# Residual and activation sums by adding transfers on GpSimd's queue, with negated blocks, and a norm into rows of its own

## Chip, cores and metric

The kernel runs on one core of one Trainium2 chip. The metric is the device time of one execution in microseconds (us); less is better. Its engines are TensorE (PE, matrix products; PEld its weight loads), VectorE (DVE), ScalarE (ACT), GpSimd (POOL) and SyncE (SP). Each works through its own instructions in order and waits for the others by semaphores. Transfers (DMA) are issued from the queue of an engine, here nearly all from SP's, and run beside the engines.

## What is computed

One decoder layer on 1024 tokens of width 1024, all in float32. Cut to the part that the change touches:

```python
m = concat([rmsnorm(a, g_attn), rmsnorm(c, g_conv)])
x = x + rmsnorm(m @ w_out, mix_post_norm)
h = rmsnorm(x, ffn_pre_norm)
f = (silu(h @ w_gate) * (h @ w_up)) @ w_down
x = x + rmsnorm(f, ffn_post_norm)
```

Here `a` is the output of an attention with low-rank queries and keys, `c` that of a gated convolution. D_FF is 2816. A last gated embedding is added behind `f`.

## The kernel before

**Precision.** Each float32 matrix is kept as two parts of a reduced type: an upper part (`split`, line 209, a cast on ACT) and the rest (line 210, a subtraction on DVE or POOL). A product is three matmuls: upper with upper, upper with lower, lower with upper. For the output projection these are lines 220 to 222, for the FFN lines 1192, 1194 and 1195.

**FFN products.** The FFN's first two matrix products use a scheme of Strassen's kind. The activations h, transposed, are a 2 x 2 arrangement of blocks of 512 x 512 (128 partitions x 2048 numbers each in memory): B11, B12, B21, B22. The weights of a pair of 128-column tiles form A11 to A22. Seven products per pair and per matrix (gate or up) take the place of eight. `ORDER` is (1, 2, 6, 5, 7, 3, 4), and `RIGHT` names the activation factor of each: product 1 takes B11, 2 B21, 3 B22, 4 T4, 5 T1, 6 T2, 7 T3. The T's are sums of blocks: T3 = B22 - B12, T2 = T3 + B11, T1 = B22 - T2, T4 = B21 - T2. `factor` builds the weight factors, on DVE for the first pair of tiles and on POOL for the others, and splits them. `product` runs 12 matmuls on PE and then gathers the result.

**Rows.** The stage around the change is a loop over t from 0 to 10. `wo_a(t)` finishes the projection of row block t (128 tokens; 24 matmuls), L1071 gathers it, and the square sum (L230 on ACT), the addition of epsilon (L226 on DVE) and the power (L227 on POOL) make the factor of its norm. `wo_x1(t - 1)` multiplies by that factor and the gain (L1077), adds the row block of x that `load_x` had brought (L1079), stores the sum (L1081, tensor x_d) and computes the factor of the second norm. `wo_n(t - 2)` multiplies the same buffer, in place, by that factor and gain (L1086). `h2_turn(t - 3)` transposes the result on PE (L1106, eight per row block; the prediction calls those of row block t "Tt"). For blocks 0 to 3, ACT copies the transposed rows into a buffer (L1108) that goes out to the tensor hr_d (L1116); their B11 and B21 are also split at once. For blocks 4 to 7 the copies (L1110) go into `tr[0]` and `tr[1]`, which are B12 and B22, and B22 is split. At t = 9, B11 and B21 come back from hr_d (L1277, L1278) into the buffers in which the lower parts of T1 and T4 will stand. `raw_load` (L1148) brings the weights, and the first products (1, of the first pair) run once the projection is done.

**Sums.** Behind the loop `t_sum` (L1303) makes the four sums on DVE, each 128 x 2048, and `t_split` splits each, among the weight factors and products that come between.

**What sets the order.** A scheduler with its own model of time puts the instructions of every engine in order; the program's text gives the dependences. Buffers come from two arenas, mem_f (30 units of 128 x 512, raw data) and mem_r (72 units, split data): the free space that has rested longest is given out next, so a load can wait for the last reader of its buffer. Matmul results stand in eight banks.

Of the kernel before, what the change touches and what calls it, by code (L numbers as in the profile page):

```python
# [8 lines left out]
F32 = mybir.dt.float32  # L9
# [126 lines left out]
def hybrid_layer(ctx: ExitStack, tc: tile.TileContext, x, x_t, p_t, cols_in, positions,  # L136
# [69 lines left out]
    def split(h, l, src, gain=None, eng=None):  # L206

        if gain is None:
            act.copy(h, src)  # L209
            (eng or dve).tensor_tensor(l, src, h.bitcast(F32), op=ALU.subtract)  # L210
# [24 lines left out]
    def bank3(ap, k):  # L235
        return ap.rearrange("p (k c) -> p k c", k=k)
# [811 lines left out]

    rows_y, rows_x = {}, {}

    def load_y(t):
        rows_y[t] = mf(2, ML)
        sp.dma_start(rows_y[t].a, y_d[t * P : (t + 1) * P, :])

    def load_x(t):
        rows_x[t] = mf(2, ML)
        sp.dma_start(rows_x[t].a, x[t * P : (t + 1) * P, :])

    def row_norm(t, i):
        r = ss_y[:, 2 * t + i : 2 * t + i + 1]
# [10 lines left out]
        row_norm(t, 0)  # L1073

    def wo_x1(t):
        y, xr = rows_y[t].a, rows_x.pop(t)
        dve.scalar_tensor_tensor(y, y, ss_y[:, 2 * t : 2 * t + 1], g_mix.a, op0=ALU.mult,  # L1077
                                 op1=ALU.mult)
        dve.tensor_tensor(y, y, xr.a, op=ALU.add)  # L1079
        free(xr)  # L1080
        sp.dma_start(x1_d[t * P : (t + 1) * P, :], y)  # L1081
        row_norm(t, 1)

    def wo_n(t):
        y = rows_y[t].a
        dve.scalar_tensor_tensor(y, y, ss_y[:, 2 * t + 1 : 2 * t + 2], g_ffn.a, op0=ALU.mult,  # L1086
                                 op1=ALU.mult)

# [2 lines left out]
    def four(b):  # L1093
        return b.a.rearrange("p (k c) -> p k c", k=4)

    def h2_turn(t):
        src = rows_y.pop(t)
        o = slice(t % 4 * P, (t % 4 + 1) * P)
        first = t < T // 2
        if first:  # L1100
            raw = mf(2, ML)
        for q in range(2):
            ids, b = ps.get()
            for j in range(4):
                k = 4 * q + j
                pe.transpose(b[:, j * P : (j + 1) * P], src.a[:, k * P : (k + 1) * P], ident[:])  # L1106
            if first:
                act.copy(raw.a[:, q * U : (q + 1) * U], b)  # L1108
            else:
                act.copy(four(tr[q])[:, :, o], bank3(b, 4))  # L1110
# [33 lines left out]
    def raw_load(fp, i, where=None):  # L1144

        for m, w in enumerate((w_gate, w_up)):
            raws[fp, m, i] = r = mf(2, where)
            sp.dma_start(r.a, w[2 * fp + i])  # L1148

    def factor(fp, m, p):  # L1150
        eng = pool if fp else dve
        a = raws[fp, m, 0].a
        a11, a12 = a[:, 0:U], a[:, U:]
        if p == 1:
            src = a11
        elif p == 2:
            src = a12
        else:
            b = raws[fp, m, 1].a
            a21, a22 = b[:, 0:U], b[:, U:]  # L1160
            if p == 6:
                eng.tensor_tensor(a21, a21, a22, op=ALU.add)
# [12 lines left out]
        h, l = wp[fp, m, p] = pair(1, RR)
        split(h.a, l.a, src)
        if p == ORDER[-1]:
            free(raws.pop((fp, m, 0)), raws.pop((fp, m, 1)))

# [74 lines left out]
    for t in range(T + 3):  # L1254
        if t < T:
            wo_a(t)
        elif t == T:
            for d in (mTa, wo):
                for h, l in d.values():
                    free(h, l)  # L1260
            for i in head[:2]:
                product(*i)
        elif t == T + 1:
            for i in head[2:]:
                product(*i)
        if 1 <= t <= T:
            wo_x1(t - 1)
        if t < T:
            load_x(t)
        if 2 <= t <= T + 1:  # L1270
            wo_n(t - 2)
        if t == T + 1:
            free(g_mix, g_ffn)
            t2 = mf(4, MG)
            tf["T1"], tf["T4"] = pair(4, BT), pair(4, BT)
            b11, b21 = tf["T1"][1].a.bitcast(F32), tf["T4"][1].a.bitcast(F32)
            sp.dma_start(b11.rearrange("p (k c) -> p k c", k=4), hr_d[:, 0:4, :])  # L1277
            sp.dma_start(b21.rearrange("p (k c) -> p k c", k=4), hr_d[:, 4:8, :])  # L1278
        if t >= 3:
            h2_turn(t - 3)  # L1280
        if t + 2 < T:
            load_y(t + 2)
        if t == T - 1:
            raw_load(0, 1, ML)
        if t == T:
            raw_load(1, 0, ML)
        if t == T // 2:
            for i in head:
                factor(*i)
    b12, b22 = tr[0], tr[1]  # L1290

    def both(f, fp, p):
        for m in range(2):
# [2 lines left out]
    def t_split(n, v):  # L1296
        if n not in tf:
            tf[n] = pair(4, BT)
        h, l = tf[n]
        split(h.a, l.a, v)  # L1300

    def t_sum(o, x, y, op):
        dve.tensor_tensor(o, x, y, op=op)  # L1303
# [314 lines left out]
```

## Time and profile before

| | |
|---|---|
| median of 3 executions | 1226.24 us (1225.47 to 1227.34) |
| the profiled execution | 1227.49 us |
| its span in the profile | 1225.4 us |
| PE busy / DVE busy / POOL busy | 1201.5 / 810.6 / 503.8 us |
| chain that ended last, share of PE | 80% |

The profile comes from one execution. A row of a timeline gives start and duration in microseconds, engine, line, operation, the memory written and read, the size, and in brackets how long the engine stood idle before and which instruction ended that. In the grouped lines the last two entries are the idle time and what ended it. The chain that ended last follows the waits back from the end; a line of the waits view sums what an engine waited for. DMA rows give the median time from issue to landing.

The stage of the loop lies between 436 and 536 us of the span. GpSimd's queue carries no transfer there; all are on SP's queue.

### The profile page before, as it was taken

To read this page: it belongs to the slowest core of one execution; us is meant where nothing else is said; L and a number is where in the kernel's file an instruction comes from. 1 tells how busy PE (TensorE), PEld (TensorE's weight loads), DVE (VectorE), ACT (ScalarE), POOL (GpSimd) and SP (SyncE) were. 2 spreads that over 40 slices of the span, in tenths; PEclk is the share of its full clock that TensorE was granted. 3 is DMA by queue.
4 is the path that set the end of the run, shared out by engine and by line. 5 is a ranking of instruction groups with operands and counts; after the bars stand their busy time and mean duration, and the time that the engine had idled before them with its cause. 6 is when DMAs were issued, how large, how long until landed. Compare 5 with 4: busy or idle time off the path is not lost.

```text
span 1225.4 us, 16706 instructions
## 1 busy us (share of the span) xinstructions
PE 1201.5 (98%) x5918; PEld 1012.2 (83%) x5918; DVE 810.6 (66%) x1173; ACT 587.3 (48%) x1079; POOL 503.8 (41%) x392
## 2 busy tenths in 40 slices
PE   8999999999999999789999999999999999999998
PEld 6998888889999888678788888888888888888886
DVE  6676346478867758785657665565556677758775
ACT  7543333267766736543433333333345546545652
POOL 4433534226554311025888646674634102202321
PEclk8999999999999999889999999999999999999999
DMA  8712553994561667524465445543566576654342
GB/s 267 258 39 104 184 202 133 278 365 90 135 161 44 232 223 252 203 104 143 161 229 197 140 144 190 178 157 118 209 209 200 184 242 230 233 172 164 120 136 79
DMA packets 89821, 217.77 MB, mean 178 GB/s; under 512 B 9030, under 2 KB 18026, under 8 KB 88426
## 3 DMA queue, kind: packets, MB, share of 16 engines
q1 hardware_dynamic: 89392, 216.17, 53.4%
q8 instruction: 46, 0.75, 0.3%
q10 hardware_dynamic: 346, 0.54, 0.2%
q14 instruction: 37, 0.30, 0.1%
HBM read 145.38 MB, written 71.04 MB: 177 GB/s over the span
## 4 chain that ended last, share of the span: by engine, by line
PE 80%; DVE 6%; DMA 5%; issue 3%; ACT 3%; POOL 2%; ACTq 0%; POOLq 0%; DVEq 0%; SPq 0%
PE banks L1192 10%; PE banks L1195 10%; PE banks L1194 10%; PE banks L220 7%; PE banks L222 7%; PE banks L221 7%; PE banks L1391 6%; PE banks L1390 6%; PE banks L1389 6%; PE banks L894 2%; DVE mem_r L210 2%; PE banks L1498 1%; PE banks L1501 1%; PE banks L1500 1%; PE banks L865 1%
## 5 line engine op out<-in xcount | busy, mean ns | idle before, releaser
L210 DVE TENSOR_TENSOR mem_r<-mem_f,mem_r 128x512 fp32r<-128x512 f32 (+1 forms) x404 | 374.4, 958 | 206.4 <-ACT mem_r L209 194.1
L209 ACT CAST mem_r<-mem_f 128x512 fp32r<-128x512 f32 (+2 forms) x407 | 258.4, 666 | 410.6 <-PE banks L1194 128.7
L1192 PE MATMUL banks<-mem_r 128*128 128x512 f32 x616 | 242.0, 393 | 4.5 <-ACT mem_r L209 3.4
L1194 PE MATMUL banks<-mem_r 128*128 128x512 f32 x616 | 241.6, 392 | 0.0
L1195 PE MATMUL banks<-mem_r 128*128 128x512 f32 x616 | 240.8, 392 | 0.1
L220 PE MATMUL banks<-mem_r 128*128 128x512 f32 (+2 forms) x536 | 196.3, 371 | 2.4 <-ACT mem_r L209 1.7
L221 PE MATMUL banks<-mem_r 128*128 128x512 f32 (+2 forms) x536 | 196.4, 368 | 1.3 <-POOL mem_r L210 1.2
L222 PE MATMUL banks<-mem_r 128*128 128x512 f32 (+2 forms) x536 | 196.0, 368 | 0.0
L1192 PEld LDWEIGHTS banks<-mem_r 128*128 128x128 f32 x616 | 116.5, 189 | 30.7 <-ACT mem_r L209 5.0
L1195 PEld LDWEIGHTS banks<-mem_r 128*128 128x128 f32 x616 | 116.7, 189 | 25.7 <-DVE mem_r L210 1.1
L1194 PEld LDWEIGHTS banks<-mem_r 128*128 128x128 f32 x616 | 116.8, 190 | 24.3 <-DVE mem_r L210 0.2
L1391 PE MATMUL banks<-mem_r 128*128 128x512 f32 x308 | 119.8, 389 | 0.0
L1390 PE MATMUL banks<-mem_r 128*128 128x512 f32 x308 | 119.8, 389 | 0.0
L1389 PE MATMUL banks<-mem_r 128*128 128x512 f32 x308 | 119.8, 390 | 0.0
L220 PEld LDWEIGHTS banks<-mem_r 128*128 128x128 f32 x536 | 101.2, 190 | 19.1 <-ACT mem_r L209 2.8
L221 PEld LDWEIGHTS banks<-mem_r 128*128 128x128 f32 x536 | 101.6, 190 | 17.4 <-POOL mem_r L210 1.4
L222 PEld LDWEIGHTS banks<-mem_r 128*128 128x128 f32 x536 | 101.5, 189 | 16.1
L879 POOL TENSOR_TENSOR mem_f<-mem_f,stats 128x640 f32<-128x640 f32 (+5 forms) x64 | 73.4, 1161 | 92.0 <-DVE stats L878 49.4
L227 POOL TENSOR_TENSOR small<-small,mhalf 128x1 f32<-128x1 f32 (+2 forms) x46 | 37.6, 821 | 177.5 <-DVE small L226 177.0
L1210 DVE TENSOR_TENSOR mem_f<-banks,mem_f 128x512 f32<-128x512 f32 x66 | 45.2, 686 | 55.9 <-PE banks L1195 55.8
L210 DVE TENSOR_TENSOR mem_r<-banks,mem_r 128x512 fp32r<-128x512 f32 (+3 forms) x118 | 69.3, 612 | 12.9 <-ACT mem_r L209 12.3
L1390 PEld LDWEIGHTS banks<-mem_r 128*128 128x128 f32 x308 | 57.8, 188 | 12.0
(197 smaller groups left out, 1890.0 us busy)
## 6 DMA issues: line engine op xcount, KB each, us to landing
sc_d<-mem_f SPq DMA_DIRECT2D x77, 256.0 KB, 3.5
mem_f<-sc_d SPq DMA_DIRECT2D x77, 256.0 KB, 3.0
mem_f<-in_w_gate_dram SPq DMA_DIRECT2D x22, 512.0 KB, 5.2
mem_f<-in_w_up_dram SPq DMA_DIRECT2D x22, 512.0 KB, 5.1
mem_f<-in_w_down_dram SPq DMA_DIRECT2D x22, 512.0 KB, 4.5
wc_d<-mem_f SPq DMA_DIRECT2D x22, 512.0 KB, 2.7
mem_f<-wc_d SPq DMA_DIRECT2D x44, 256.0 KB, 3.1
mem_f<-in_w_down_dram SPq DMA_DIRECT2D x33, 256.0 KB, 3.4
```

What stands on the lines that cost most here:

```text
L209: act.copy(h, src)
L210: (eng or dve).tensor_tensor(l, src, h.bitcast(F32), op=ALU.subtract)
L220: pe.matmul(o, wh, vh, start=i == 0, stop=False)
L221: pe.matmul(o, wh, vl, start=False, stop=False)
L222: pe.matmul(o, wl, vh, start=False, stop=i == n - 1)
L879: pool.tensor_tensor(pt.a[:, 0:n], pt.a[:, 0:n], sm.to_broadcast([P, n]), op=ALU.mult)
L1192: pe.matmul(b, wh.a[:, c], th[:, k], start=first and k == 0, stop=False, skip_group_check=True)
L1194: pe.matmul(b, wh.a[:, c], tl[:, k], start=False, stop=False, skip_group_check=True)
L1195: pe.matmul(b, wl.a[:, c], th[:, k], start=False, stop=k == 3, skip_group_check=True)
L1389: pe.matmul(b, ah.a[:, c], bh.a, start=first, stop=False, skip_group_check=True)
L1390: pe.matmul(b, ah.a[:, c], bl.a, start=False, stop=False, skip_group_check=True)
L1391: pe.matmul(b, al.a[:, c], bh.a, start=False, stop=last, skip_group_check=True)
```

## The change

The row of x is no longer loaded and added on DVE. A transfer on GpSimd's queue reads x from the chip's memory and adds it into the row in place. The second norm writes into rows of its own (`rows_n`), and the first buffer is freed behind it. The sums of activation blocks are four adding transfers on the same queue, between buffers on the chip: b11 += b12, b12 += b22, b22 += b11, b21 += b22. An adding transfer only adds, so blocks off the diagonal (B12, B21) are kept as negatives: ACT multiplies by 1 or -1 where it copied. With that, b12 becomes T3, b22 becomes T2, b11 becomes -T1 and b21 becomes -T4. The weight factors of products 4 and 5 are negated as they are split (L1180 on ACT, L1181 on DVE). The buffer `t2` is gone, the row loads of the projection stand elsewhere in the loop, `raw_load` of two weight halves may use fewer units, and the splits stand later in the text.

```diff
@@ rows and norms
-    def load_x(t):
-        rows_x[t] = mf(2, ML)
-        sp.dma_start(rows_x[t].a, x[t * P : (t + 1) * P, :])
...
     def wo_x1(t):
-        y, xr = rows_y[t].a, rows_x.pop(t)
+        y = rows_y[t].a
         dve.scalar_tensor_tensor(y, y, ss_y[:, 2 * t : 2 * t + 1], g_mix.a, op0=ALU.mult,
                                  op1=ALU.mult)
-        dve.tensor_tensor(y, y, xr.a, op=ALU.add)
-        free(xr)
+        pool.dma_start(y, x[t * P : (t + 1) * P, :], accum_op=ALU.add)
         sp.dma_start(x1_d[t * P : (t + 1) * P, :], y)
         row_norm(t, 1)
 
+    rows_n = {}
+
     def wo_n(t):
-        y = rows_y[t].a
-        dve.scalar_tensor_tensor(y, y, ss_y[:, 2 * t + 1 : 2 * t + 2], g_ffn.a, op0=ALU.mult,
-                                 op1=ALU.mult)
+        y = rows_y.pop(t)
+        rows_n[t] = mf(2, ML)
+        dve.scalar_tensor_tensor(rows_n[t].a, y.a, ss_y[:, 2 * t + 1 : 2 * t + 2], g_ffn.a,
+                                 op0=ALU.mult, op1=ALU.mult)
+        free(y)
@@ h2_turn
-        src = rows_y.pop(t)
+        src = rows_n.pop(t)
...
+            f = -1.0 if q == first else 1.0
             if first:
-                act.copy(raw.a[:, q * U : (q + 1) * U], b)
+                act.mul(raw.a[:, q * U : (q + 1) * U], b, f)
             else:
-                act.copy(four(tr[q])[:, :, o], bank3(b, 4))
+                act.mul(four(tr[q])[:, :, o], bank3(b, 4), f)
@@ factor
-        split(h.a, l.a, src)
+        if p in (4, 5):
+
+            act.mul(h.a, src, -1.0)
+            dve.scalar_tensor_tensor(l.a, src, -1.0, h.a.bitcast(F32), op0=ALU.mult,
+                                     op1=ALU.subtract)
+        else:
+            split(h.a, l.a, src)
@@ the loop over t
-        if t + 2 < T:
-            load_y(t + 2)
+        if 1 <= t < T - 1:
+            load_y(t + 1)
         if t == T - 1:
-            raw_load(0, 1, ML)
+            raw_load(0, 1, ((0, 18),))
         if t == T:
-            raw_load(1, 0, ML)
+            raw_load(1, 0, ((0, 18),))
@@ the sums
-    t_sum(b12.a, b22.a, b12.a, ALU.subtract)
+
+    for o, v in ((b11, b12), (b12, b22), (b22, b11), (b21, b22)):
+        pool.dma_start(o, v, accum_op=ALU.add)
     both(factor, 1, 1)
     both(product, 1, 1)
-    t_sum(t2.a, b12.a, b11, ALU.add)
-    t_split("T3", b12.a)
-    free(b12)
-    raw_load(2, 0)
     both(factor, 1, 2)
     both(product, 1, 2)
-    t_split("T2", t2.a)
-    both(factor, 0, 6)
-    t_sum(b22.a, b22.a, t2.a, ALU.subtract)
+    raw_load(2, 0)
+    t_split("T3", b12)
     both(factor, 2, 1)
     both(product, 2, 1)
-    t_split("T1", b22.a)
-    free(b22)
     both(factor, 2, 2)
     both(product, 2, 2)
+    t_split("T2", b22)
+    both(factor, 0, 6)
+    t_split("T1", b11)
     both(factor, 0, 5)
-    t_sum(t2.a, b21, t2.a, ALU.subtract)
     factor(0, 0, 7)
-    t_split("T4", t2.a)
-    free(t2)
+    t_split("T4", b21)
+    free(*tr.values())
```

Three places show the order in which instructions now stand. First DVE around the norm of row block 6 and the second multiplication of row block 7. Before, with L1077 and L1079 of block 7 and L1086 of block 6; L1162, L1163 and L1171 are sums of up weights for product 6 of the first pair:

```order
L1077 SCALAR_TENSOR_TENSOR mem_f<-mem_f,small 128x1024
L210 TENSOR_TENSOR mem_r<-banks,mem_r 128x4x128
L1210 TENSOR_TENSOR mem_f<-banks,mem_f 128x512
L1079 TENSOR_TENSOR mem_f<-mem_f 128x1024
L1210 TENSOR_TENSOR mem_f<-banks,mem_f 128x512
L1214 TENSOR_TENSOR mem_f<-mem_f 128x512
L1086 SCALAR_TENSOR_TENSOR mem_f<-mem_f,small 128x1024
L226 TENSOR_SCALAR small<-small 128x1
L1162 TENSOR_TENSOR mem_f<-mem_f 128x512
L1163 TENSOR_TENSOR mem_f<-mem_f 128x512
L1171 TENSOR_TENSOR mem_f<-mem_f 128x512
L210 TENSOR_TENSOR mem_r<-mem_f,mem_r 128x512 x2
```

The same place on DVE now. L1164, L1165 and L1173 are the same sums for the gate weights, which now come second, L226 belongs to block 7's first norm or block 6's second, L1074 is block 7's multiplication, L1085 the norm of block 6:

```order
L226 TENSOR_SCALAR small<-small 128x1
L1164 TENSOR_TENSOR mem_f<-mem_f 128x512
L226 TENSOR_SCALAR small<-small 128x1
L1074 SCALAR_TENSOR_TENSOR mem_f<-mem_f,small 128x1024
L1165 TENSOR_TENSOR mem_f<-mem_f 128x512
L1085 SCALAR_TENSOR_TENSOR mem_f<-mem_f,small 128x1024
L1173 TENSOR_TENSOR mem_f<-mem_f 128x512
L1218 TENSOR_TENSOR mem_f<-banks,mem_f 128x512
```

The second set of weight sums stood behind block 6's norm and block 7's multiplication. Its first row now stands ahead of both, so it must have its weights before the two rows go on.

Second, SP's queue at the same place. Here L1077 stores a row of the residual sum (row block 5 first), L1118 stores block 3 to hr_d, L1150 behind it loads the gate weights that the L1164 above reads, into the buffer that the hr_d stores read, and L1284 and L1285 bring hr_d back:

```order
L1077 DMA x_d<-mem_f 128x1024
L1118 DMA hr_d<-mem_f 1024x1x128
L1150 DMA mem_f<-in_w_gate_dram 128x1024
L1284 DMA mem_r<-hr_d 128x2048
L1285 DMA mem_r<-hr_d 128x2048
L1077 DMA x_d<-mem_f 128x1024
L1150 DMA mem_f<-in_w_up_dram 128x1024
L1150 DMA mem_f<-in_w_gate_dram 128x1024
L1077 DMA x_d<-mem_f 128x1024
```

Before, this load of gate weights stood ahead of the hr_d stores of blocks 2 and 3 (L1116), in a buffer that no such store reads:

```order
L1081 DMA x_d<-mem_f 128x1024
L1148 DMA mem_f<-in_w_gate_dram 128x1024
L1116 DMA hr_d<-mem_f 1024x1x128
L1081 DMA x_d<-mem_f 128x1024
L1055 DMA mem_f<-y_d 128x1024
L1116 DMA hr_d<-mem_f 1024x1x128
L1059 DMA mem_f<-in_x_dram 128x1024
L1277 DMA mem_r<-hr_d 128x2048
```

Third, the sums. POOL's queue from the last rows of x on, where L1076 is the adding transfer of a row and the four L1311 are the sums that make -T1, T3, T2 and -T4; behind them stands the first of the sums of the down weights:

```order
L1076 DMA mem_f<-in_x_dram 128x1024
L227 TENSOR_TENSOR small<-small,mhalf 128x1 x3
L1076 DMA mem_f<-in_x_dram 128x1024
L227 TENSOR_TENSOR small<-small,mhalf 128x1
L1311 DMA mem_r<-mem_f 128x2048
L1311 DMA mem_f<-mem_f 128x2048
L1311 DMA mem_f<-mem_r 128x2048
L1311 DMA mem_r<-mem_f 128x2048
L1248 TENSOR_TENSOR mem_f<-mem_f 128x512
```

And DVE where the lower parts of the sums are made; the rows of 128x2048 are those of T3, T1 (in place) and T2:

```order
L1222 TENSOR_TENSOR mem_f<-mem_f 128x512
L210 TENSOR_TENSOR mem_r<-mem_f,mem_r 128x2048
L210 TENSOR_TENSOR mem_r<-mem_f,mem_r 128x512
L210 TENSOR_TENSOR mem_r<-mem_r 128x2048
L210 TENSOR_TENSOR mem_r<-mem_f,mem_r 128x512
L210 TENSOR_TENSOR mem_r<-mem_f,mem_r 128x2048
```

The four sums have moved from DVE to POOL's queue, one behind the other, and T1's lower part stands ahead of T2's, where T2's came first.

More of the change, by code (lines that the diff above doesn't have):

```diff
@@ L1047, in hybrid_layer @@
     brow(ffn_pre_norm, D, g_ffn)
-    rows_y, rows_x = {}, {}
+    rows_y = {}
     def load_y(t):
@@ L1267, in hybrid_layer @@
             wo_x1(t - 1)
-        if t < T:
-            load_x(t)
+        if t == T:
+            free(g_mix)
         if 2 <= t <= T + 1:
@@ L1272, in hybrid_layer @@
         if t == T + 1:
-            free(g_mix, g_ffn)
-            t2 = mf(4, MG)
+            free(g_ffn)
             tf["T1"], tf["T4"] = pair(4, BT), pair(4, BT)
@@ L1289, in hybrid_layer @@
                 factor(*i)
-    b12, b22 = tr[0], tr[1]
+    b12, b22 = tr[0].a, tr[1].a
     def both(f, fp, p):
@@ L1300, in t_split @@
         split(h.a, l.a, v)
-    def t_sum(o, x, y, op):
-        dve.tensor_tensor(o, x, y, op=op)
-    t_sum(b12.a, b22.a, b12.a, ALU.subtract)
+    for o, v in ((b11, b12), (b12, b22), (b22, b11), (b21, b22)):
+        pool.dma_start(o, v, accum_op=ALU.add)
     both(factor, 1, 1)
     both(product, 1, 1)
-    t_sum(t2.a, b12.a, b11, ALU.add)
-    t_split("T3", b12.a)
-    free(b12)
-    raw_load(2, 0)
     both(factor, 1, 2)
     both(product, 1, 2)
-    t_split("T2", t2.a)
-    both(factor, 0, 6)
-    t_sum(b22.a, b22.a, t2.a, ALU.subtract)
+    raw_load(2, 0)
+    t_split("T3", b12)
     both(factor, 2, 1)
     both(product, 2, 1)
-    t_split("T1", b22.a)
-    free(b22)
     both(factor, 2, 2)
     both(product, 2, 2)
+    t_split("T2", b22)
+    both(factor, 0, 6)
+    t_split("T1", b11)
     both(factor, 0, 5)
-    t_sum(t2.a, b21, t2.a, ALU.subtract)
     factor(0, 0, 7)
-    t_split("T4", t2.a)
-    free(t2)
+    t_split("T4", b21)
+    free(*tr.values())
     facc = []
```

## Prediction

> **What bounds the kernel now.** The page's busy times come first.
>
> ```profile
> PE 1201.5 (98%) x5918; PEld 1012.2 (83%) x5918; DVE 810.6 (66%) x1173; ACT 587.3 (48%) x1079; POOL 503.8 (41%) x392
> ```
>
> TensorE (PE) is busy for 1201.5 of 1225.4 us, so taking work off VectorE (DVE) pays only where PE waits or runs slowly. The windows view shows where: start and end, length, busy time and count of PE, weight loads, DVE, ACT and POOL, then granted clock, DMA share and GB/s.
>
> ```profile
> 486.00:496.00 10.00, 10.00 (x48) 8.28 (x48) 8.99 (x12) 7.01 (x13) 1.27 (x3) 1.00 0.60 176
> 496.00:506.00 10.00, 2.66 (x13) 2.07 (x12) 5.47 (x9) 1.99 (x4) 0.87 (x1) 0.72 1.01 385
> 506.00:516.00 10.00, 9.66 (x40) 7.70 (x39) 8.20 (x10) 6.30 (x12) 0.06 (x1) 0.76 0.44 163
> 516.00:526.00 10.00, 6.88 (x29) 5.07 (x28) 10.00 (x10) 6.61 (x7) 0.00 (x0) 0.92 0.17 53
> 526.00:536.00 10.00, 10.00 (x35) 7.98 (x34) 8.77 (x7) 5.31 (x7) 0.00 (x0) 0.74 0.07 28
> 536.00:546.00 10.00, 10.00 (x46) 8.29 (x45) 7.75 (x8) 4.93 (x9) 3.38 (x3) 1.00 0.48 157
> ```
>
> Until 496 and after 536 PE is full at clock 1.00. Between them it loses time twice, and runs at 0.72 to 0.92 in and after each gap. PE's timeline has both (start, duration, what it waited for):
>
> ```profile
> 494.65 0.39 PE L1195 MATMUL banks<-mem_r 128*128 128x512 f32 x1
> ...
> 497.37 0.39 PE L1195 MATMUL banks<-mem_r 128*128 128x512 f32 x1
> 505.09 1.94 PE L1106 MATMUL banks<-ident,mem_f 128*128 128x128 f32 x8 [7.34 <-issue]
> 507.37 0.79 PE L1192 MATMUL banks<-mem_r 128*128 128x512 f32 x1 [0.34 <-ACT mem_r L209]
> 507.96 0.63 PE L1194 MATMUL banks<-mem_r 128*128 128x512 f32 x1
> ...
> 511.78 1.03 PE L1106 MATMUL banks<-ident,mem_f 128*128 128x128 f32 x8
> 512.57 0.48 PE L1192 MATMUL banks<-mem_r 128*128 128x512 f32 x1
> ...
> 525.31 0.79 PE L1192 MATMUL banks<-mem_r 128*128 128x512 f32 x1 [3.09 <-ACT mem_r L209]
> 525.90 0.63 PE L1194 MATMUL banks<-mem_r 128*128 128x512 f32 x1
> 526.33 0.63 PE L1195 MATMUL banks<-mem_r 128*128 128x512 f32 x1
> ...
> 536.14 0.39 PE L1192 MATMUL banks<-mem_r 128*128 128x512 f32 x1
> ```
>
> At full clock matmuls start 0.227 apart (12 from 494.65 to 497.37); behind the gaps 0.43 apart (525.90 to 526.33), for 8 matmuls after the first and 13 after the second. The first gap ends with the transposes of row block 6 (T6, 505.09), those of block 7 (T7) follow at 511.78; the second is a late weight cast. Together that is about 16 us: 7.3 + 0.3 + 3.1 waited, 21 x 0.2 = 4.2 for slow matmuls, 1.94 - 0.79 = 1.1 for slow transposes. Product 6, the first reader of T2, begins at about 536.1. All later matmuls are the same work, so **the sum compares the moment when product 6 can run**.
>
> Why T6 is late stands on DVE's timeline:
>
> ```profile
> 478.01 1.28 DVE L1077 SCALAR_TENSOR_TENSOR mem_f<-mem_f,small 128x1024 f32<-128x1024 f32 x1 [0.66 <-POOL small L227]
> 494.31 1.28 DVE L1077 SCALAR_TENSOR_TENSOR mem_f<-mem_f,small 128x1024 f32<-128x1024 f32 x1 [0.67 <-POOL small L227]
> 496.71 1.22 DVE L1079 TENSOR_TENSOR mem_f<-mem_f 128x1024 f32<-128x1024 f32 x1
> 503.71 1.28 DVE L1086 SCALAR_TENSOR_TENSOR mem_f<-mem_f,small 128x1024 f32<-128x1024 f32 x1 [4.39 <-DMA x_d<-mem_f]
> 504.97 0.68 DVE L1162 TENSOR_TENSOR mem_f<-mem_f 128x512 f32<-128x512 f32 x1
> 508.56 1.28 DVE L1086 SCALAR_TENSOR_TENSOR mem_f<-mem_f,small 128x1024 f32<-128x1024 f32 x1
> 513.86 2.29 DVE L1303 TENSOR_TENSOR mem_f<-mem_f 128x2048 f32<-128x2048 f32 x1 [0.77 <-ACT mem_f L1110]
> ```
>
> Block 6's norm (L1086, in place) waited 4.39 us for the store of the row that it overwrites. Block 7's, queued behind, came at 508.56. The four activation sums are L1303, the first at 513.86.
>
> **The change part by part.** Durations of this stage come from the grouped lines (busy, mean ns), landings from the DMA issues of 430 to 540 (count, KB, median us), where three rows are of the whole span: wc_d, sc_d and wo_d.
>
> ```profile
> L1079 DVE TENSOR_TENSOR mem_f<-mem_f 128x1024 f32<-128x1024 f32 x8 | 9.7, 1218 | 0.0
> L230 ACT ACTIVATE mem_r<-mem_f 128x1024 fp32r<-128x1024 f32 x16 | 17.0, 1063 | 25.4 <-DVE mem_f L1071 20.7 <-DVE mem_f L1079 4.7
> L230 ACT ACTIVATION_READ_ACCUMULATOR mem_r<-mem_f 128x1 f32 x16 | 3.0, 187 | 0.0
> L210 DVE TENSOR_TENSOR mem_r<-mem_f,mem_r 128x2048 fp32r<-128x2048 f32 x4 | 9.1, 2285 | 1.6 <-ACT mem_r L209 1.6
> L209 ACT CAST mem_r<-mem_f 128x2048 fp32r<-128x2048 f32 x4 | 7.6, 1910 | 1.9 <-DVE mem_f L1303 1.9
> mem_f<-in_x_dram SPq DMA_DIRECT2D x7, 512.0 KB, 4.1
> hr_d<-mem_f SPq DMA_DIRECT2D x4, 512.0 KB, 6.4
> mem_f<-in_w_gate_dram SPq DMA_DIRECT2D x3, 512.0 KB, 5.3
> mem_f<-in_w_up_dram SPq DMA_DIRECT2D x4, 512.0 KB, 8.0
> wc_d<-mem_f SPq DMA_DIRECT2D x22, 512.0 KB, 2.7
> sc_d<-mem_f SPq DMA_DIRECT2D x77, 256.0 KB, 3.5
> mem_r<-wo_d SPq DMA_DIRECT2D x4, 1024.0 KB, 12.7
> ```
>
> *Removed.* Eight L1079 (9.7 us) and four L1303 (2.29 each, 9.2 us) leave DVE, eight x loads leave SP's queue, and the norm no longer waits for the row's store. None of the 18.9 us is PE's: it counts only through T6, T7 and T2.
>
> *Negatives.* ACT's copies become multiplications by -1 of the same size, and in the weight splits of products 4 and 5 a subtract becomes a scalar-tensor-tensor. Like forms show no price: L1077 with a scalar and a gain, 1.28, against L1079's 1.22. I take nothing, 0.06 each at most.
>
> *The adding transfers are not in the trace of before.* The x add (512 KB, name its landing A) reads x and the row and writes the row. From below it costs what a load of this size does, 4.1, or 2.7 on a quiet queue (wc_d); a gain over that is excluded, as it moves no less. From above stands the slowest group of this size in the stage, w_up's 8.0, and more if transfers collide. I take half as much again as the quiet copy for the second read, 4.1, times 4.1/2.7 for this stage's traffic: 6.2; **A = 6.5** with the issue. An activation sum (1 MB in SBUF, landing S) has below it 4.1 (2.7 and another 512 KB at 1.4), above it wo_d's 12.7. With the second read, another 2.8, S = 6.9, and **S = 7.1** with the issue: nearer the low end, because the DMA share there is 0.17 and 0.07, not 1.01.
>
> The Trainium skill, "Collectives: The Full Stack", section "The bandwidth ceiling: the fold count and why AG ≠ RS ≠ AR", says that an adding transfer reads two sources through one ring and halves the rate (62.28 against 32.35 GB/s). By that ratio, as an estimate, S would be 4.1 x 1.93 = 7.9 and the sum 2.4 us more. No run here shows it.
>
> *Rows.* Row 5's L1077 stood at 478.01; without the adds ahead of it its successor comes 0.9 earlier, 477.1. It ends at 478.4, its add lands at 484.9, and SP, in order, issues the row's store and then the hr_d store of block 3 at 485.4. A weight load (gate, half 1) has that store's buffer: 485.4 + 6.4 = 491.8, + 5.3 = 497.1. On DVE its first sum (L1164, 0.68 as L1162) stands ahead of the rstd of block 6 and of row 7's L1074: that starts at 497.9, where before it was at 494.31. Behind it L1165 and block 6's norm: 497.9 + 1.28 + 0.68 + 1.28 = 501.1 for T6, **4.0 earlier** than 505.09. Row 7's add is issued at 499.2; in the stretch with DMA share 1.01 I give it 7.0, landed 506.2. Square 1.06 + 0.19, rstd 0.8 (GpSimd's half is the wait of 0.67 ahead of 494.31) and norm 1.28 make 509.5: T7 starts **2.3 earlier**. PE, however, has run dry before T7 (T6 until 503.0, then the 12 matmuls that took 507.37 to 511.78 before, 4.4, until 507.5), so its eight transposes cost 1.9, like T6's, not 0.8: end 511.4 against 512.57, 1.2 earlier.
>
> *Sums.* Each needs the one before it, so all four stand in a chain on GpSimd's queue. Block 7's copies on ACT release the first at 511.1. They land at 518.2, 525.3, 532.4 and 539.5. T2 is the third. DVE takes the lower part of T1 first, in place in the buffer that the third sum reads, then a weight piece, then T2's: 532.4 + 2.2 + 0.6 + 2.2 = 537.4. Before, T2 was an L1303 at 516.67 and a split behind it. GpSimd (0.00 busy from 516 to 536) is blocked meanwhile and loses nothing. ACT's casts of T1 and T3 wait for sums 1 and 2 with weight casts behind them, done by 520.8 and 527.9, where PE wants them at 522.7 and 530.7.
>
> *Sum.* After T7, 94 matmuls at 0.227 take 21.3, with 1.6 for slow ones: PE is at product 6 at 534.3, does two matmuls on T2's upper part and stands until 537.4. As a start of product 6 that is 536.9, **0.8 behind** 536.1. The wait, 2.6, is like the one of 3.09 after which 13 matmuls took 0.2 too much each, so I add the same **2.6**. The second gap of before (late weights) goes, since those loads start behind T5 to T7. In all +3.4: 1227.49 becomes 1230.9 for a profiled execution; these are 1.25 above the median, so 1226.24 + 3.4 = **1229.6**.
>
> **The rivals.**
>
> *Cheap adds.* With A = S = 4.1 row 5's add lands at 482.5, the weights at 494.7, L1074 of row 7 starts at 495.5, T6 at 498.7 and T7 at 505.0; the sums give T2 at 505.6 + 12.3 + 5 = 522.9, before PE needs it at 505.9 + 22.3 = 528.2. That is 8 before 536.1: **1218**. For it: the queue is nearly empty after 516. Against: a second read must be paid somewhere.
>
> *Dear adds (slower).* T2 comes at three times S behind T7, and S beyond about 6.2 goes to the end threefold. S = 9.5 gives 3.4 + 7.2, **1237**; S = 12.7, 3.4 + 16.8, **1246**. For it: wo_d's row. Against: that row's traffic came out of HBM beside others.
>
> *GpSimd's issue is held up by DVE.* GpSimd and DVE already stand in each other's way where both read SBUF:
>
> ```profile
> 542.46 1.80 POOL L1240 TENSOR_TENSOR mem_f<-mem_f 128x512 f32<-128x512 f32 x1 [36.41 <-DVE mem_r L210]
> 544.35 1.29 POOL L1241 TENSOR_TENSOR mem_f<-mem_f 128x512 f32<-128x512 f32 x1
> ```
>
> ```profile
> 544.43 1.76 DVE L210 TENSOR_TENSOR mem_r<-mem_f,mem_r 128x512 fp32r<-128x512 f32 x1
> ```
>
> DVE's L210, a size that took 0.68 in L1162, took 1.76 until GpSimd's L1241 was done, and L1240 took 1.80 against 1.29. If an issue waits for the running DVE operation, at most 2.29, then at DVE's load of 8 to 10 tenths about 1 each, three ahead of T2: 3.4 + 3, **1233**. The Trainium skill, "SBUF — State Buffer", section "SBUF: two separate sides", has that rule: GpSimd's writing of descriptors stands still while DVE holds the shared port. No row here shows it for a DMA.
>
> *An even trade.* With S at 6.2 or less, and A as forecast, T2 is in time (511.1 + 18.6 + 5 = 534.7) and product 6 runs at 534.3, 1.8 before 536.1: **1224.4**, within the 0.2%.
>
> **How the numbers follow.** The forecast with its neighbours (A 6 to 7.5, S 6.6 to 8.5) has 0.34, even trade 0.14, cheap 0.24, dear 0.20, held up 0.08. The range goes from the cheap adds, 1217, to the dear ones' end, 1246. A measurement of this kernel tells 0.2%, 2.45 us, from no change: faster is below 1223.8, slower above 1228.7. Faster gets cheap, 0.05 of even trade and 0.01 of the forecast: 0.30. Same gets the rest of even trade, 0.09, 0.10 of the forecast and 0.01 of held up: 0.20. Slower gets dear, 0.23 of the forecast and 0.07 of held up: 0.50.
>
> **What would show it.** T6 and T7 at 501 and 509, an x add of 6.5 and a sum of 7.1 in the DMA issues, and a wait of PE at 534.7 for L210 of T2. If sums land in under 5, no PE wait stands there; if DVE holds issues up, the gap between two sums is longer than their landings. The forecast is wrong above all if S is: 1 us of it is 3 us of the end.

## The result and the profile after

The changed kernel takes 1238.81 us in the median of 5 runs (1237.57 to 1241.15) beside 1226.24 (1225.47 to 1227.48) before: ratio 1.0103, 95% interval 1.0089 to 1.0118. It is **12.6 us slower**; the forecast was 3.4, in a range to 1246. The profiled execution took 1238.81, its span is 1237.0.

The busy times of the page after, to be read against those of before:

```profile
PE 1202.1 (97%) x5918; PEld 1012.2 (82%) x5918; DVE 795.2 (64%) x1161; ACT 587.6 (48%) x1079; POOL 516.6 (42%) x404
```

DVE lost 15.4 us of work, TensorE has the same amount, and the span grew by 11.6: what was freed was not what the end waited for. The windows view (columns as before) shows where:

```profile
466.00:476.00 10.00, 8.44 (x45) 6.67 (x44) 5.08 (x8) 2.30 (x4) 1.99 (x3) 1.00 1.02 269
476.00:486.00 10.00, 8.91 (x42) 6.87 (x41) 6.31 (x9) 6.31 (x13) 2.87 (x4) 1.00 0.94 283
486.00:496.00 10.00, 6.14 (x24) 4.61 (x23) 7.67 (x12) 6.40 (x13) 2.83 (x4) 0.80 0.97 240
506.00:516.00 10.00, 2.62 (x16) 2.06 (x14) 4.46 (x8) 3.10 (x7) 1.06 (x2) 0.83 0.95 306
536.00:546.00 10.00, 7.66 (x32) 5.56 (x30) 6.94 (x5) 5.56 (x8) 0.86 (x1) 1.00 0.78 157
```

Before, PE was full until 496. Now it waits from 466 on. The DMA engines are busy for 1.02, 0.94, 0.97 and 0.95 of the stretches at 466, 476, 486 and 506 (0.96, 0.91, 0.60 and 0.44 before), and DVE, which was at 8.2 to 9.0 of 10 there, is at 4.5 to 7.7: it waits too. PE's timeline around the transposes of blocks 6 and 7 and at product 6:

```profile
507.59 1.03 PE L1106 MATMUL banks<-ident,mem_f 128*128 128x128 f32 x8
517.04 0.80 PE L1200 MATMUL banks<-mem_r 128*128 128x512 f32 x1 [8.42 <-ACT mem_r L209]
517.64 0.63 PE L1202 MATMUL banks<-mem_r 128*128 128x512 f32 x1
518.07 1.91 PE L1106 MATMUL banks<-ident,mem_f 128*128 128x128 f32 x8
...
543.84 0.51 PE L1200 MATMUL banks<-mem_r 128*128 128x512 f32 x1 [1.18 <-ACT mem_r L209]
544.84 0.49 PE L1200 MATMUL banks<-mem_r 128*128 128x512 f32 x1 [0.49 <-ACT mem_r L209]
547.10 0.80 PE L1202 MATMUL banks<-mem_r 128*128 128x512 f32 x1 [1.77 <-DVE mem_r L210]
```

T6 is at 507.59 (forecast 501.1) and T7 at 518.07 (forecast 509.5). Product 6 would have begun at 546.65, had its first two matmuls not gone ahead (547.10 less two of 0.227): 10.5 behind the 536.1 of before, where the forecast had 0.8. Of the 11.6 by which the span grew, about 1 more is slow matmuls behind that last wait. What product 6 waited for stands on ACT, the cast of T2, and on DVE, where T1's lower part goes ahead of T2's:

```profile
541.88 1.91 ACT L209 CAST mem_r<-mem_f 128x2048 fp32r<-128x2048 f32 x1 [4.24 <-DMA mem_f<-mem_r]
```

```profile
541.95 2.29 DVE L210 TENSOR_TENSOR mem_r<-mem_r 128x2048 fp32r<-128x2048 f32 x1 [2.42 <-DMA mem_f<-mem_r]
```

The landings of the DMA issues, in the stretch 430 to 560, with the two queues above them (packets, MB, share of 16 engines):

```profile
q1 hardware_dynamic: 8955, 18.69, 41.8%
q0 software_dynamic: 1728, 8.39, 34.7%
...
mem_f<-in_x_dram POOLq DMA_DIRECT2D x8, 512.0 KB, 6.1
...
mem_r<-hr_d SPq DMA_DIRECT2D x2, 1024.0 KB, 8.9
mem_r<-mem_f POOLq DMA_DIRECT2D x2, 1024.0 KB, 6.9
```

Both estimates of a landing were near: 6.1 in the median for an x add (6.5 with its issue), 6.9 for a sum (7.1). The median hides what decides: the single rows. GpSimd's timeline shows when each transfer was issued,

```profile
460.49 0.89 POOL L1076 DMA_DIRECT2D mem_f<-in_x_dram  x1 [1.88 <-DVE mem_f L1074]
466.66 0.88 POOL L1076 DMA_DIRECT2D mem_f<-in_x_dram  x1 [1.86 <-DVE mem_f L1074]
...
505.97 0.88 POOL L1076 DMA_DIRECT2D mem_f<-in_x_dram  x1 [0.15 <-issue]
...
520.05 0.89 POOL L1311 DMA_DIRECT2D mem_r<-mem_f  x1 [3.70 <-ACT mem_f L1112]
527.61 0.86 POOL L1311 DMA_DIRECT2D mem_f<-mem_f  x1 [6.67 <-DMA mem_r<-mem_f]
534.90 0.86 POOL L1311 DMA_DIRECT2D mem_f<-mem_r  x1 [6.43 <-DMA mem_f<-mem_f]
542.14 0.86 POOL L1311 DMA_DIRECT2D mem_r<-mem_f  x1 [6.38 <-DMA mem_f<-mem_r]
```

and ACT's the square sums (L230) and copies that waited for landings:

```profile
470.32 1.06 ACT L230 ACTIVATE mem_r<-mem_f 128x1024 fp32r<-128x1024 f32 x1 [4.39 <-DMA mem_f<-in_x_dram]
...
476.29 0.60 ACT L1110 ACTIVATE mem_f<-banks 128x512 f32<-128x512 f32 x1 [2.19 <-DMA hr_d<-mem_f]
...
478.21 1.09 ACT L230 ACTIVATE mem_r<-mem_f 128x1024 fp32r<-128x1024 f32 x1
...
514.36 1.06 ACT L230 ACTIVATE mem_r<-mem_f 128x1024 fp32r<-128x1024 f32 x1 [4.80 <-DMA mem_f<-in_x_dram]
...
516.36 2.19 ACT L209 CAST mem_r<-mem_f 128x512 fp32r<-128x512 f32 x4
```

Row 2's add, issued at 460.49, landed at 470.2: 9.7 us. SP, in order, stored that row and only then sent block 0's rows out:

```profile
470.25 0.32 SPq L1077 DMA_DIRECT2D x_d<-mem_f  x1
470.62 0.58 SPq L1118 DMA_DIRECT2D hr_d<-mem_f  x1
...
473.19 0.32 SPq L1077 DMA_DIRECT2D x_d<-mem_f  x1
```

Block 1's copy on ACT (476.29) waited for that hr_d store, because all four blocks go out through one buffer, and the square sum of row 3, landed by 473.2, stood behind the copy until 478.21. Row 7's add took from 505.97 to 514.36, 8.4, among the reloads of hr_d; four weight casts (516.36) stand behind its square sum on ACT, and these are PE's 8.42 us. In both of these adds the first part was standing still. From 460.6 to 464.3 and from 506.2 to 510.0, behind the two issues, the DMA view shows no packet of GpSimd's queue, q0, but SP's queue at work:

```profile
q1 hardware_dynamic: 211, 0.80, 77.9%
```

```profile
q1 hardware_dynamic: 258, 1.26, 93.2%
```

The adds of rows 4 to 6, which landed 5.4 to 5.8 after their issue, moved their first packets about 1.6 after it; those of rows 2 and 7 about 4.1 after it.

DVE's timeline shows where the multiplications (L1074) of rows 5 and 7 stood, and the wait of L1164 for the gate weights ahead of row 7:

```profile
482.81 1.29 DVE L1074 SCALAR_TENSOR_TENSOR mem_f<-mem_f,small 128x1024 f32<-128x1024 f32 x1 [0.66 <-POOL small L227]
...
503.47 0.69 DVE L1164 TENSOR_TENSOR mem_f<-mem_f 128x512 f32<-128x512 f32 x1 [4.13 <-DMA mem_f<-in_w_gate_dram]
...
504.14 1.28 DVE L1074 SCALAR_TENSOR_TENSOR mem_f<-mem_f,small 128x1024 f32<-128x1024 f32 x1
```

### The profile page after: what moved, and what is told of

Read it like the earlier page. It is cut to its first block, busy times and chain, and to the rows that moved or that the text cites. A ratio compares the mean times of both kernels' runs of the same rounds, so it can differ in the third digit from the quotient of the medians.

```text
span 1237.0 us, 16728 instructions
## 1 busy us (share of the span) xinstructions
PE 1202.1 (97%) x5918; PEld 1012.2 (82%) x5918; DVE 795.2 (64%) x1161; ACT 587.6 (48%) x1079; POOL 516.6 (42%) x404
## 3 DMA queue, kind: packets, MB, share of 16 engines
q0 software_dynamic: 1728, 8.39, 3.6%
## 4 chain that ended last, share of the span: by engine, by line
PE 77%; DMA 9%; issue 5%; DVE 4%; ACT 3%; POOL 2%; SPq 0%; POOLq 0%; DVEq 0%; ACTq 0%
PE banks L1203 10%; PE banks L1200 10%; PE banks L1202 10%; PE banks L220 6%; PE banks L221 6%; PE banks L222 6%; PE banks L1391 6%; PE banks L1390 6%; PE banks L1392 6%; PE banks L894 2%; DMA hr_d<-mem_f 1%; PE banks L1502 1%; ACT mem_r L209 1%; PE banks L1501 1%; PE banks L1499 1%
## 5 line engine op out<-in xcount | busy, mean ns | idle before, releaser
L210 DVE TENSOR_TENSOR mem_r<-mem_f,mem_r 128x512 fp32r<-128x512 f32 (+1 forms) x358 | 327.9, 949 | 173.7 <-ACT mem_r L209 163.2
L209 ACT CAST mem_r<-mem_f 128x512 fp32r<-128x512 f32 (+1 forms) x361 | 227.8, 665 | 347.1 <-PE banks L1202 82.2
L1200 PEld LDWEIGHTS banks<-mem_r 128*128 128x128 f32 x616 | 117.1, 190 | 40.1 <-ACT mem_r L209 15.6
L1202 PEld LDWEIGHTS banks<-mem_r 128*128 128x128 f32 x616 | 117.3, 190 | 26.8 <-DVE mem_r L210 2.3
L1203 PEld LDWEIGHTS banks<-mem_r 128*128 128x128 f32 x616 | 116.8, 190 | 24.4 <-DVE mem_r L210 0.3
L220 PEld LDWEIGHTS banks<-mem_r 128*128 128x128 f32 x536 | 100.8, 189 | 22.9 <-ACT mem_r L209 3.2
L221 PEld LDWEIGHTS banks<-mem_r 128*128 128x128 f32 x536 | 101.3, 189 | 17.1 <-POOL mem_r L210 1.3
L222 PEld LDWEIGHTS banks<-mem_r 128*128 128x128 f32 x536 | 101.1, 189 | 16.2
L210 DVE TENSOR_TENSOR mem_r<-banks,mem_r 128x512 fp32r<-128x512 f32 (+3 forms) x118 | 69.5, 613 | 17.2 <-ACT mem_r L209 16.6
L1181 DVE SCALAR_TENSOR_TENSOR mem_r<-mem_f,mem_r 128x512 fp32r<-128x512 f32 x44 | 43.1, 987 | 43.4 <-ACT mem_r L1180 43.4
```

The costliest lines, as they stand in the source:

```text
L220: pe.matmul(o, wh, vh, start=i == 0, stop=False)
L221: pe.matmul(o, wh, vl, start=False, stop=False)
L222: pe.matmul(o, wl, vh, start=False, stop=i == n - 1)
L1200: pe.matmul(b, wh.a[:, c], th[:, k], start=first and k == 0, stop=False, skip_group_check=True)
L1202: pe.matmul(b, wh.a[:, c], tl[:, k], start=False, stop=False, skip_group_check=True)
L1203: pe.matmul(b, wl.a[:, c], th[:, k], start=False, stop=k == 3, skip_group_check=True)
```

## The experiments

Each edit is to the changed kernel where nothing else is said, and each ratio is to the kernel before on the same chip. Lines of the kernels differ by a few.

**e1: x on DVE, sums as transfers.**

```diff
-        pool.dma_start(y, x[t * P : (t + 1) * P, :], accum_op=ALU.add)
+        xr = rows_x.pop(t)
+        dve.tensor_tensor(y, y, xr.a, op=ALU.add)
+        free(xr)
...
+        if t < T:
+            load_x(t)
```

> The changed kernel, but the row of x is loaded on SP's queue and added on DVE as before; the four sums stay adding transfers. Theory A (the loss of 12.6 us is made by the rows: each x add lands late, the residual's store waits for it on SP's queue, and the hr_d stores, the weight loads and ACT's copies stand behind): the transposes of block 7 come back from 518 to 510 or earlier and the time to 1226-1231. Theory B (the chain of four sums at 7.3 us makes the loss): little changes, 1235-1239. Either way PE waits about 2 to 4 us for T2 if the transposes come early.

1228.37 us, ratio 1.0030 (1.0017 to 1.0043). T7 came at 505.8. PE then waited for T2:

```profile
534.04 1.22 PE L1206 MATMUL banks<-mem_r 128*128 128x512 f32 x2 [4.31 <-ACT mem_r L209]
537.30 0.79 PE L1208 MATMUL banks<-mem_r 128*128 128x512 f32 x1 [2.04 <-DVE mem_r L210]
```

**e2: sums on DVE, x as transfers.**

```diff
-    for o, v in ((b11, b12), (b12, b22), (b22, b11), (b21, b22)):
-        pool.dma_start(o, v, accum_op=ALU.add)
+    t_sum(b12, b12, b22)
+    t2 = mf(4)
...
+    t_sum(t2.a, b12, b11)
...
+    t_sum(b22, t2.a, b22, ALU.subtract)
...
+    t_sum(t2.a, b21, t2.a)
```

> The changed kernel, but the four sums are DVE operations again, with one buffer more, placed as before; the x adds stay transfers. Theory A: T6 and T7 stay at 507 and 518 and the time stays at 1233-1238, 1 to 5 us better than the changed kernel. Theory B: 1224-1228.

1234.82 us, ratio 1.0080 (1.0059 to 1.0102), T7 at 517.4: almost where it is with the sums as transfers, as theory A had it. The time is 0.0023 under the changed kernel's, with overlapping intervals.

**e3: both on DVE** (the edits of e1 and e2).

> The changed kernel with both additions on DVE again, so that only the norm into rows of its own, the negatives and the moved loads are left. If the two kinds of adding transfer are all of the loss, 1218-1227, under before by up to what the norm's wait of 4.39 us held back. If the moved loads and the one buffer for all hr_d stores are part of it without any adding transfer, over 1228.

1222.04 us, ratio 0.9977 (0.9966 to 0.9988), T7 at 505.8. So the norm into rows of its own, the negatives and the moved loads together gain about 2.8 us; the x adds cost 0.0103 of the time from there (e2), the sums 0.0053 (e1), both together 0.0126. T7 stands in the same place in e1 and e3, and in e2 and the changed kernel: the x adds make T7 late, the sums act only behind it.

**e4: plain copies.**

```diff
-        pool.dma_start(y, x[t * P : (t + 1) * P, :], accum_op=ALU.add)
+        pool.dma_start(y, x[t * P : (t + 1) * P, :])
...
-        pool.dma_start(o, v, accum_op=ALU.add)
+        pool.dma_start(o, v)
```

> The changed kernel with each of the twelve adding transfers turned into a plain copy of the same size on the same queue, so the additions of x and of the activation sums are left out. If the second read makes the adding transfers slow, a 1 MB copy lands in 4 to 5 us instead of 6.9 and the x rows in 4 instead of 6.1, and the time falls to 1220-1229. If GpSimd's queue and its issue are slow in themselves, copies land as late as adds and the time stays above 1235.

1225.32 us, ratio 1.0005 (0.9993 to 1.0016), T7 at 510.6. The DMA rows of e4, 430 to 560:

```profile
q0 software_dynamic: 1728, 8.39, 19.2%
...
mem_f<-in_x_dram POOLq DMA_DIRECT2D x8, 512.0 KB, 5.2
...
mem_r<-mem_f POOLq DMA_DIRECT2D x2, 1024.0 KB, 4.8
```

Both kinds of addition are left out here. Queue, bytes and the order on every engine are the same. It is adding that costs: the same 8.39 MB take 34.7% of the engines as adds and 19.2% as copies, 1.81 times as much. By row, the copies of x landed in 3.9 to 7.2, the adds in 5.4 to 9.7.

**e5: four buffers for hr_d.**

```diff
-            raw = mf(2, ML)
+            raw = tr[t // 2].a[:, t % 2 * 2 * U : (t % 2 * 2 + 2) * U]
```

> The changed kernel with one edit: the transposed rows of blocks 0 to 3, which all went out to hr_d through one buffer, get four buffers of their own (the space where blocks 4 to 7 are written later). Theory A1 (each of ACT's copies waits for the hr_d store of the block before, and the square sums of the next rows stand behind it on ACT, so the rows come every 7.65 us and not every 6.2; the gate weights then wait for the same buffer): ACT's 6.3 us of waits for hr_d and DVE's 4.1 for the weights go, block 6's norm (505.9) comes 5 to 8 earlier, and the time falls by 5 to 9 us to 1229-1234 beside 1226. Theory A2 (the landing of the x adds alone paces the rows): under 2 us of change.

1242.57 us, ratio 1.0133 (1.0106 to 1.0159), T7 at 519.7: no faster than the changed kernel (the intervals overlap), against A1. ACT's waits for hr_d went in blocks 0 to 3 (one of 4.8 came up at block 4, which is written into the same space), and PE stays full until 476, but with more transfers at once each lands later. Windows view and DMA rows of e5:

```profile
466.00:476.00 10.00, 10.00 (x49) 8.34 (x49) 7.65 (x11) 6.74 (x15) 2.64 (x5) 1.00 1.03 276
```

```profile
mem_f<-in_x_dram POOLq DMA_DIRECT2D x8, 512.0 KB, 7.0
...
hr_d<-mem_f SPq DMA_DIRECT2D x4, 512.0 KB, 8.2
```

The x adds take 7.0 instead of 6.1, the hr_d stores 8.2 instead of 6.1, and the rows are no earlier in the end.

**e6: the residual's store on ACT's queue.**

```diff
-        sp.dma_start(x1_d[t * P : (t + 1) * P, :], y)
         row_norm(t, 1)
+        act.dma_start(x1_d[t * P : (t + 1) * P, :], y)
```

> The changed kernel with the residual's store issued from ACT's queue behind the square sum that waits for the same add, so that SP's queue is not held up by an x add. If the hold-up of SP (the first hr_d store stood 4.7 us behind it) is the cost: 4 to 6 us off, 1232-1235. If the one buffer's turn (hr_d store 6.1 and two copies 1.5) sets the pace of 7.65 by itself: under 3 us off.

1237.18 us, ratio 1.0083 (1.0060 to 1.0107), T7 at 515.4: 0.0020 or 2.5 us under the changed kernel, with overlapping intervals, as the second theory had it; but e5 speaks against that theory's reason, since four buffers gave nothing back. The x adds landed in 7.4.

**e7: e5 and e6 together.**

> Both edits, four hr_d buffers and the residual's store on ACT's queue, with all twelve adds still transfers. If buffer and queue order are all that the x adds cost, T6 and T7 come as I forecast (501 and 509.5) or earlier and what is left is the wait for T2: 1226-1231. If the adds' landings are left as a cost, 1231-1236.

1242.31 us, ratio 1.0132 (1.0108 to 1.0155), T7 at 520.2. A miss of both theories: neither buffers nor the queue's order give the time back.

**e8: e3 with four hr_d buffers.**

> Both additions on DVE (as in e3), norm in rows of its own, negatives, and four hr_d buffers. If the single buffer costs nothing without the adds, the time of e3 (0.2% under before); if it holds rows up there too, 2 to 5 us less, 1217-1221 beside 1226.

1220.48 us, ratio 0.9951 (0.9932 to 0.9970), T7 at 504.8. Where no adding transfer is in the rows, the same edit as in e5 does no harm: about 3 us under e3, with intervals that just meet. **This version beats both kernels.**

**e9: without the residual's stores.**

```diff
-        sp.dma_start(x1_d[t * P : (t + 1) * P, :], y)
         row_norm(t, 1)
...
-        sp.dma_start(j.a, x1_d[t * P : (t + 1) * P, :])
+        sp.dma_start(j.a, x[t * P : (t + 1) * P, :])
```

> The changed kernel without the eight stores of the residual rows (the end of the kernel reads x in their place, so that the second residual lacks the first one): all twelve adds stay. New theory, after e5: the DMA engines themselves are full between 456 and 506 (shares of 0.82 to 1.02), and an adding transfer takes 1.8 times a copy's share of them, so taking away any 4 MB of other transfers gives the loss back, whichever queue or buffer they use. Then x adds land in 5 or less (6.1 now), PE's waits of 1.2 to 2.1 ahead of the row blocks' matmuls go, and the time falls by 5 to 10 us, ratio 1.002 to 1.006. If the adds' own latency paces the rows, or the buffers do, it stays over 1.008.

1231.25 us, ratio 1.0041 (1.0026 to 1.0056), T7 at 510.7: 0.0062 or 7.6 us come back, as expected, but not through the landings: the median is 6.4, and the adds of rows 3, 4, 5 and 7 landed in 9.1, 8.0, 7.4 and 9.2, each later than in the changed kernel (6.5, 5.8, 5.4 and 8.4). Row 2's add is followed by row 4's 13.9 us later (459.39 and 473.29 on GpSimd) instead of 16.0, and row 7's is issued at 497.71, not 505.97. The edit takes away two things at once, 4 MB of traffic and the place on SP's queue where a store waits for an add: block 0's hr_d store goes out at 463.28, not 470.62. Moving that store to another queue gave 2.5 us (e6); how the rest divides is not shown.

**e10: e3 with every residual row stored twice.**

```diff
         sp.dma_start(x1_d[t * P : (t + 1) * P, :], y)
+        sp.dma_start(x2_d[t * P : (t + 1) * P, :], y)
```

> The kernel of e3 (both additions on DVE) with each residual row stored twice, the second time to memory that nothing reads: 4 MB of plain stores more, about 12 us of all DMA engines, which is what turning the x loads into adds cost them. If full DMA engines made the loss, the time goes from 0.998 of before to 1.003-1.009 with no adding transfer in the kernel. If it is the adds' latency or GpSimd's issue, it stays below 1.001.

1223.19 us, ratio 0.9981 (0.9972 to 0.9991): no different from e3. The windows view of e10:

```profile
466.00:476.00 10.00, 10.00 (x50) 8.37 (x49) 7.39 (x10) 4.25 (x10) 2.06 (x2) 1.00 0.99 343
486.00:496.00 10.00, 7.81 (x27) 5.94 (x27) 6.63 (x10) 5.54 (x11) 1.59 (x3) 0.83 0.93 323
496.00:506.00 10.00, 6.28 (x32) 5.01 (x31) 8.21 (x13) 5.22 (x8) 0.15 (x1) 0.99 1.01 417
```

The DMA engines are as full as in the changed kernel, T7 stands at 508.2, only 2.4 behind e3, and the time does not suffer. Full engines alone are not the cause either.

**e11: T3 and T2 on DVE, T1 and T4 as transfers**, in the kernel of e8.

```diff
+    dve.tensor_tensor(t2.a, b12, b22, op=ALU.add)
...
+    dve.tensor_tensor(b22, t2.a, b11, op=ALU.add)
+    pool.dma_start(b11, b12, accum_op=ALU.add)
...
+    pool.dma_start(b21, b22, accum_op=ALU.add)
```

> The kernel of e8 (x added on DVE, own rows, four hr_d buffers), but of the four sums only T3 and T2, which PE wants first, are on DVE; those of T1 and T4 are adding transfers, issued where their 7 us lie beside products. In e8 DVE is full from 506 to 526 and PE loses 4.8 us there. If the transfers cost only where something waits for them, this is e8 or up to 3 us better, 1217-1221 beside 1226; if they cost in any place, 1223 or more.

1225.93 us, ratio 1.0001 (0.9990 to 1.0012): 0.0050 worse than e8, so the transfers cost here too. The two were issued 0.8 apart and ran one behind the other; they landed 7.2 and 13.6 after their issue. ACT cast T1 at 521.32 and then stood until T4 had landed, though product 4, the reader of T4, is the last of the seven. The weight casts on ACT and splits on DVE stand behind T4's, and PE waited for them at 531 and 534:

```profile
514.15 1.06 POOL L1322 DMA_DIRECT2D mem_r<-mem_f  x1 [14.70 <-DVE mem_f L1321]
514.91 1.21 POOL L1330 DMA_DIRECT2D mem_r<-mem_f  x1
```

```profile
521.32 1.90 ACT L209 CAST mem_r<-mem_r 128x2048 fp32r<-128x2048 f32 x1 [3.78 <-DMA mem_r<-mem_f]
528.52 1.90 ACT L209 CAST mem_r<-mem_r 128x2048 fp32r<-128x2048 f32 x1 [5.30 <-DMA mem_r<-mem_f]
```

```profile
530.99 0.80 PE L1205 MATMUL banks<-mem_r 128*128 128x512 f32 x1 [2.71 <-ACT mem_r L209]
534.47 0.80 PE L1208 MATMUL banks<-mem_r 128*128 128x512 f32 x1 [2.26 <-DVE mem_r L210]
```

**e12: one weight load later.**

```diff
-        if t == T - 1:
-            raw_load(0, 1, ((0, 18),))
         if t == T:
             raw_load(1, 0, ((0, 18),))
+        if t == T + 1:
+            raw_load(0, 1, ((0, 18),))
```

> The changed kernel with one load moved: the second weight half of the first pair (the load whose first sum stood ahead of row 7's multiplication on DVE and waited 4.1 us for it) is issued two steps of the loop later, behind the load for product 1 of the second pair. If the weight gate is the step that I mis-sized, row 7's L1074 goes from 504.1 to 499-500, its add is issued 5 earlier, PE's wait of 8.4 us ahead of T7 shrinks by 4 or more, and the time falls by 4 to 7 us, ratio 1.004-1.007. If row 7's add only meets the reloads of hr_d and the other weight loads sooner and lands no earlier, the ratio stays over 1.009.

1244.70 us, ratio 1.0155 (1.0126 to 1.0183), T7 at 524.7. The first half came true: L1074 of row 7 stood at 499.17 and its add was issued at 501.01, five earlier. It landed only three earlier, 10.4 after its issue. Then ACT waited in its own order for another weight load, and row 7's square sum behind it:

```profile
513.79 0.62 ACT L209 CAST mem_r<-mem_f 128x512 fp32r<-128x512 f32 x1 [6.92 <-DMA mem_f<-in_w_gate_dram]
...
516.26 1.08 ACT L230 ACTIVATE mem_r<-mem_f 128x1024 fp32r<-128x1024 f32 x1
```

The wait moved from DVE to ACT and grew.

## Where the forecast was right, and which term was mis-sized

**Direction, mechanism of the sums.** Right. The kernel is slower, and the sums alone make it so: e1, with no other adding transfer, takes 1.0030 of before. The sums ran one behind the other, 7.56, 7.29 and 7.24 apart (S was 7.1), T2's upper part was cast at 541.88, and PE waited 1.18 + 0.49 + 1.77 = 3.4 for T2 (forecast 2.6). The slow matmuls behind the last wait took five steps of 0.43, about 1 too much (forecast 2.6). In e1, where T7 is early, the same chain costs 6.35 us of waiting: the price of the sums grows as the rows get faster.

**The size.** Not right: 12.6 where 3.4 was forecast. The range held the time because it reached to the end of the dear adds, 1246. Those had S at 9.5 to 12.7, and S was 7.0 here; that the time stands beside their 1237 is luck.

**The weight gate.** The mechanism was right: DVE's L1164 waited 4.1 us for the gate weights ahead of row 7. The gate opened at 503.47, not at 497.1.

**The rows: the mis-sized term.** T7 came 8.6 us later than forecast (518.07 against 509.5), and that is the difference between 3.4 and 12.6 but for 0.6; the forecast had T7 2.3 earlier than before, and it came 6.3 later. The step that failed is the chain from row 5's L1077 "0.9 earlier", which kept the pace of the rows of before and gave the adds of the rows ahead no part in it, and with it "A = 6.5" used as one number for each row. Row 5's multiplication stood at 482.81, not 477.1, block 3's hr_d store went out at 493.39, not 485.4, and row 7's multiplication stood at 504.14, not 497.9: 6.2 of the 8.6. Row 7's landing, 8.4 instead of 7.0, is 1.4 more. Two things were left out. Traffic: single adds took 9.7 and 8.4 us. And the instructions that queue behind a late add: SP's hr_d store behind the row's store, ACT's copy behind that store's buffer, the next square sum behind the copy.

**Why the landing counts at all.** DVE's order puts the end of row t's norm ahead of row t + 2's multiplication, so two rows share one loop: multiplication 1.28 and 0.55 to the issue, the add, and at least 4.7 us from its landing to the next multiplication (row 2: landed 470.2, next L1074 at 474.95; in e5, where the rows are closer, 480.2 and 485.35, 5.1). PE needs 24 matmuls of 0.227 and eight transposes, 0.8, for a row: 6.2 us, 12.5 for two, which by this estimate leaves 5.6 to 6.0 for the add. Copies at 5.2 in the median (e4) fit, and PE lost only 0.5 us there until 496; adds at 6.1 in the median, and 9.7 in row 2, do not. In rows 3 to 5 the queues add to it: the square sums started 3.5 to 5.0 after their adds had landed, behind ACT's copies. On DVE the same addition took 1.22, and x was loaded long before: that load's landing (4.3 to 4.4 in e1, e3 and e10) stood in no loop, and in e10 4 MB more of traffic beside it cost nothing. That the loop is what turns the landing into lost time is argued from these orders and times; no run changed the loop alone.

**What was ruled out.** The twelve issues on GpSimd took 0.86 to 1.07 each, those of e4's copies 0.53 to 0.77. Sum 4's, at 542.14, took 0.86 while DVE ran its L210 over 2048 elements (541.95 to 544.24): no hold-up by DVE is seen, and the Trainium skill's rule in "SBUF — State Buffer", section "SBUF: two separate sides", did not show for this operation. The page ties that rule to operations of DVE that run in a 2-port mode; no run here shows whether this one does. Cheap adds are out: 1 MB took 6.9, not 4.1. Buffers and queue order (e5, e6, e7, e12) were part of where the time stood, not of what it cost: each removed wait came back elsewhere, but for the 2.5 us of e6, which are not clear of the noise.

**Over the runs** T7 and the time go together, in each group by itself:

| | T7 | ratio |
|---|---|---|
| sums as transfers: e1, e9, e6 | 505.8, 510.7, 515.4 | 1.0030, 1.0041, 1.0083 |
| after, e5, e7, e12 | 518.1, 519.7, 520.2, 524.7 | 1.0103, 1.0133, 1.0132, 1.0155 |
| sums on DVE: e8, e3, e10 | 504.8, 505.8, 508.2 | 0.9951, 0.9977, 0.9981 |
| before, e2 | 511.8, 517.4 | 1, 1.0080 |

The 0.0053 between e1 and e3, with T7 in one place, is the price of the sums themselves where the rows are early; where they are late it is 0.0023 (e2 and the changed kernel), not clear of the noise. The rest of the loss goes with T7. Two runs belong to no group: e4, with copies in place of all adds, has T7 at 510.6 and 1.0005; e11, with two of the sums as transfers, has T7 at 503.1 and 1.0001.

**Open.** The adds of rows 2 and 7 moved nothing for 4.1 us while SP's transfers had the engines; in rows 4 to 6, with SP's transfers under way as well, it was 1.6. What decides when an add gets its turn is not settled, nor how the 7.6 us of e9 divide between traffic and SP's queue; and whether a third row in flight would hide the landings was not tried.

## What to carry to other kernels

An operation of 1.2 us on a busy engine is not replaced by a transfer of 6 because the engine has other work: ask whether the result stands in a loop, and how much room that loop has. Here it was some 6 us by estimate, and a load that nothing waits for became a landing that everything waits for. A landing inside a loop is to be priced at the slowest that full DMA engines give, and each queue behind the waiting instructions belongs to the price.

## What the runs showed of the hardware

An adding transfer took 1.81 times the DMA time of a copy of the same bytes (34.7% against 19.2% of the engines), where the Trainium skill ("Collectives: The Full Stack", section "The bandwidth ceiling: the fold count and why AG ≠ RS ≠ AR") has 1.93 for reducing collectives. One behind the other, sums of 1 MB landed in 6.9 to 7.0 (changed kernel) or 6.9 to 8.9 (e1), and copies in 4.4 to 5.0 (e4). Two adds of 1 MB issued 0.8 apart on GpSimd's queue did not share the time: they landed 7.2 and 13.6 after their issue (e11). An add of 512 KB moved its first packet 1.6 after its issue in rows 4 to 6 and 4.1 after it in rows 2 and 7 of the changed kernel.
